# Rotary embedding worked in place in PSUM, early query and key pairs, in a two-layer decoder trunk

## The chip, the core and the metric

The kernel runs on one core of one Trainium2 chip. Its metric is the device time of one execution in microseconds (us); the median of three runs is the figure that counts. A core has TensorE (PE in the profile), VectorE (DVE), ScalarE (ACT), GpSimd (POOL) and SyncE (SP), which here only issues DMAs. Each works through its own instructions in order and waits on semaphores for the others. SBUF is the working memory; PSUM is the small memory into which TensorE writes, cut here into eight banks of 128 x 512 fp32.

## What is computed

The reference is a two-layer decoder over 512 tokens of width 1024, in fp32. Layer 0 (even) has four differential and eight forgetting attention heads. Layer 1 (odd) is a sparse attention: a light indexer scores all causal keys, each query keeps its 128 best, and 16 heads attend over those. Both layers end in a squared-ReLU MLP. Cut to what the change touches:

```python
def partial_rope(x, cos, sin):                 # first 16 of 64 dims of a head
    x1, x2, xp = xf[..., :half], xf[..., half:ROT_DIM], xf[..., ROT_DIM:]
    return concatenate([x1 * cos - x2 * sin, x2 * cos + x1 * sin, xp])
...
q, k, v, iq, ik, iw = _split(h @ w_in, ODD_WIDTHS)      # odd layer
ik = partial_rope(layernorm(ik, ln_g, ln_b))
logits = einsum('bqhd,bkd->bqhk', iq, ik) * IDX_DIM ** -0.5
score = einsum('bqhk,bqh->bqk', relu(logits), iw)
_, idx = lax.top_k(score, k_sel)
```

## The kernel before, in words

**Products.** Every fp32 matrix is split into a high part (a cast to fp32r on ACT) and a low part (a subtraction on DVE, or on POOL for some weights): `split`, lines 174 to 176. A projection of one block of 128 output columns is 24 matmuls of 128x512: high by high, high by low, low by high for each of eight slices of the depth (`gemm_steps`, lines 348 to 350). Its result stands in a PSUM bank of the ring `pg`, which has three banks (`B_PG`); the third block after it takes the same bank, once every instruction that reads it is over. Weights come as `raw` tiles over SP's queue in the order of a list (`full_plan`), two such tiles in flight, and are split when the block before is begun.

**Rope.** A query or key block is finished in `qk_fin` (402). `rope_from` (379) makes a copy with the rows swapped (stream_shuffle, 381), multiplies the block by the cosines (382) and the copy by the sines (383), and adds (384), all on DVE; `csr` holds the tables, already scaled by the token's norm (235). Then `split` makes the high and low parts, and `halves` (400) moves 64-row halves between tiles by DMAs on SP's queue, so that two heads can be multiplied side by side. The layer-0 heads with rope are the first four query and four key blocks; layer 1 ropes all eight of each, four index query blocks and the index key.

**Odd layer.** `odd` (841) first projects the index key and the index weights (844), turns them to tokens (851), normalises the key tile by tile (855 to 869; the power of -1/2 runs on POOL, 865), turns it back, ropes and splits it. Then four index query blocks are projected (877). From there `weave` merges generators by their progress: the index scores (`index_steps`, four head pairs by three query tiles, in the two banks of `pS`) beside the first steps of V, then the top-k (`topk_round`, 16 rounds of a maximum of eight and a replacement on each of three query tiles, lines 905 and 906, on DVE) beside the rest of V and the first two query and key pairs (`QK_EARLY`). V blocks don't use DVE. The loop of nine follows: scores of head pair i, softmax, the product with V of pair i-1, and the projection of pair i+2. A final reordering sets each engine's order from expected times, so the order on an engine isn't wholly that of the code.

Of the kernel before, what the change touches and what calls it, by code (L numbers as in the profile page):

```python
# [14 lines left out]
OP = mybir.AluOpType  # L15
# [33 lines left out]
OD_K = [0] * 8 + [6]  # L49
IDX_COVER = 12  # L50
DVE_ODD = 6
# [5 lines left out]
def rope_rows():  # L57
    pos = np.arange(S, dtype=np.float32)
    inv = (np.float32(THETA) ** (-(np.arange(0, ROT, 2, dtype=np.float32)) / np.float32(ROT))).astype(np.float32)
    ang = (pos[None, :] * inv[:, None]).astype(np.float32).astype(np.float64)  # L60
    c, s = np.cos(ang), np.sin(ang)
    t = np.zeros((2, P, S), np.float64)
    t[0] = 1.0
    for b in (0, HD):
        t[0, b:b + 8] = c
        t[0, b + 8:b + 16] = c
        t[1, b:b + 8] = -s
        t[1, b + 8:b + 16] = s
    return t.astype(np.float32)
# [7 lines left out]
def trunk(ctx, tc, x, norm_mix, w_in_even, b_forget, lambda_q1, lambda_k1, lambda_q2, lambda_k2,  # L77
# [226 lines left out]
    def full_plan():  # L304
# [13 lines left out]
        for s in range(2):  # L318
            stage(w, 0, 3 * D + s * WC)
        for u_ in range(4):  # L320
            stage(w, 0, 2 * D + u_ * WC, lo=nc.gpsimd)
        for i in range(8):
            for a in range(2):
                stage(w, 0, a * D + i * P, P, lo=nc.gpsimd)
        out_stages(w_out_odd[0], 0, 1, nc.gpsimd)
# [52 lines left out]

    def rope_from(src, tab):
        u, v = scr(), scr()  # L380
        nc.vector.stream_shuffle(v, src, SHUF)
        nc.vector.tensor_mul(u, src, tab[:, 0])
        nc.vector.tensor_mul(v, v, tab[:, 1])  # L383
        nc.vector.tensor_add(u, u, v)
        return u

# [454 lines left out]
    def odd(ap, gh):  # L841
        w = w_in_odd[0]
        fq, fk = qk_fin(ap, True, False), qk_fin(ap, True, True)
        iwt = wnext(w, 0, 3 * D + S)
# [5 lines left out]
        for t in range(NT):  # L850
            nc.tensor.transpose(p[:, t * P:t * P + HD + 8], ikf[:HD + 8, t * P:(t + 1) * P], ident[:HD + 8, :HD + 8])
        iw = ap.tile([P, NT, 8], F32, name="iw")
        xh = scr()
        pk = pT()
        for t in range(NT):
            rt = rtm[:, t:t + 1]
            nc.vector.tensor_scalar(iw[:, t], p[:, t * P + HD:t * P + HD + 8], rt, 8 ** -0.5, op0=OP.mult, op1=OP.mult)
            kr = small(HD)
            nc.vector.tensor_scalar(kr, p[:, t * P:t * P + HD], rt, None, op0=OP.mult)
            b6 = small(6)  # L860
            mv = small(4)
            nc.vector.bn_stats(b6, kr)
            nc.vector.bn_aggr(mv[:, 0:2], b6)
            nc.vector.tensor_scalar(mv[:, 2:3], mv[:, 1:2], EPS, None, op0=OP.add)
            nc.gpsimd.tensor_tensor(mv[:, 3:4], mv[:, 2:3], nhalf[:, 0:1], op=OP.pow)
            for s in range(2):
                nc.vector.tensor_scalar(xh[:, t * P + s * HD:t * P + (s + 1) * HD], kr, mv[:, 0:1], mv[:, 3:4],
                                        op0=OP.subtract, op1=OP.mult)
            nc.tensor.transpose(pk[:, t * P:(t + 1) * P], xh[:, t * P:(t + 1) * P], ident)
        kl = scr()  # L870
        nc.vector.tensor_scalar(kl, pk, cols[:, 41:42], cols[:, 42:43], op0=OP.mult, op1=OP.add)
        cs = blk("P", 4, (P, 2, S), pool=ap)
        nc.gpsimd.dma_start(cs, rope.rearrange("a p s -> p a s"))
        ky = rope_from(kl, cs)
        ikb = (blk("qk", QK_BUFS, dt=F32R, pool=ap), blk("qk", QK_BUFS, dt=F32R, pool=ap))
        split(ikb[0], ikb[1], ky)
        iq = proj(w, gh, 3 * D, fq) + proj(w, gh, 3 * D + WC, fq)

# [6 lines left out]
        def index_steps():  # L885
            for hp in range(4):
                for t in range(1, NT):
                    wd = (t + 1) * P
                    a = sc[t - 1]
                    sp = [pS(), pS()]  # L890
                    for m in range(2):
                        nc.tensor.matmul(sp[m][:, :wd], iq[hp][m][:, t * P:wd], ikb[0][:, :wd], start=True, stop=False)
                        nc.tensor.matmul(sp[m][:, :wd], iq[hp][m][:, t * P:wd], ikb[1][:, :wd], start=False, stop=True)
                    for m in range(2):
                        rl = scr()
                        nc.scalar.activation(rl[:, :wd], sp[m][:, :wd], AF.Relu, scale=HD ** -0.5)
                        nc.vector.scalar_tensor_tensor(a, rl[:, :wd], iw[:, t, 2 * hp + m:2 * hp + m + 1], a,  # L897
                                                       op0=OP.mult, op1=OP.add)
# [13 lines left out]
        vfin = v_fin(ap, 9, False, True)  # L912
        vs, qs, ks, res = [], [], [], []

# [3 lines left out]

        def v_steps():
            for i in range(8):  # L920
                yield from block_steps(w, gh, 2 * D + i * P, vfin, vs.append)
# [6 lines left out]
        def chain(*gens):  # L928
            for g in gens:
                yield from g  # L930

        def take(g, n):
            for _ in range(n):
                if next(g, g) is g:
                    return
                yield

        first = chain(v_steps(), *(qk_steps(i) for i in range(QK_EARLY)))
        weave((take(first, IDX_COVER), IDX_COVER), (index_steps(), 12))
        weave((first, 72 + 18 * QK_EARLY - IDX_COVER), (topk_steps(), 16))  # L940
        while vlate:
# [64 lines left out]
```

## Time and profile before

| | us |
|---|---|
| median of three runs (lowest, highest) | 1295.77 (1295.64, 1297.23) |
| profiled execution: time | 1293.84 |
| profiled execution: span of the instructions | 1292.1 |
| TensorE busy | 1259.1 |
| VectorE busy | 751.8 |
| ScalarE busy | 559.3 |
| GpSimd busy | 107.8 |

The odd layer's own stretch runs from about 616 us (index key projection) to about 900. The rows of the profile give start and duration in us, engine, line and operation, then what is written, an arrow, and what is read; the bracket at the end of a row holds the engine's idle time before it and what ended that. Group rows give count, busy time in us, mean duration in ns, and idle time before.

### The profile page before, as it was taken

Reading aid. Unit: us, or ns where it says so; the run is one execution under the profiler, and the core shown is the slowest. Engines: PE = TensorE matmul, PEld = TensorE weight load, DVE = VectorE, ACT = ScalarE, POOL = GpSimd, SP = SyncE. Lnnn points to the kernel's source line nnn. Section 1 sums busy time; section 2 is a strip of 40 time slices with the busy share of each in tenths; the row PEclk is TensorE's granted clock in tenths of the full one; section 3 lists DMA queues with packets and bytes.
Section 4 is the critical chain, followed back from the end, with each engine's and each line's share of the span. In section 5 each row is a group of like instructions: output and inputs, shape, how many; then the busy total and the mean of one; then the engine's idle time right before and its main releaser. Section 6 shows DMA issues by size and latency. Waiting matters only on the chain.

```text
span 1292.1 us, 15546 instructions
## 1 busy us (share of the span) xinstructions
PE 1259.1 (97%) x5874; PEld 1032.5 (80%) x5874; DVE 751.8 (58%) x1397; ACT 559.3 (43%) x1013; POOL 107.8 (8%) x80
## 2 busy tenths in 40 slices
PE   7999999999999999999989899999999999999998
PEld 6878888888888888888778677777888888888887
DVE  7997569464422344343789978888654332444233
ACT  5556667353311233332255258686443311333232
POOL 2000000000000000000326422230000000000000
PEclk9999999999999999999989899999999999999999
DMA  8645453333222233233241454532333223332211
GB/s 261 148 127 133 111 139 103 98 98 98 98 99 94 90 94 102 100 114 126 92 113 52 125 139 100 145 94 97 99 98 98 98 98 98 98 98 98 98 65 65
DMA packets 145898, 138.92 MB, mean 108 GB/s; under 512 B 7480, under 2 KB 130528, under 8 KB 145824
## 3 DMA queue, kind: packets, MB, share of 16 engines
q1 hardware_dynamic: 144576, 136.14, 35.4%
q10 hardware_dynamic: 720, 1.12, 0.3%
q0 software_dynamic: 528, 0.67, 0.3%
q8 instruction: 46, 0.75, 0.2%
q14 instruction: 28, 0.23, 0.1%
HBM read 111.18 MB, written 6.29 MB: 91 GB/s over the span
## 4 chain that ended last, share of the span: by engine, by line
PE 76%; DVE 14%; ACT 5%; issue 2%; DMA 2%; POOL 0%; SPq 0%; DVEq 0%; POOLq 0%; ACTq 0%
PE pg L348 23%; PE pg L350 23%; PE pg L349 23%; DVE sel L906 2%; ACT P L479 2%; DVE sm L905 2%; DVE scr L383 2%; PE pT L505 1%; DVE sel L897 1%; DVE PT L176 1%; DMA raw<-in_w_in_even_dram 1%; ACT P L492 1%; DVE qk L176 1%; DMA qk<-qk 1%; PE pS L471 1%
## 5 line engine op out<-in xcount | busy, mean ns | idle before, releaser
L175 ACT CAST whl<-raw 128x1024 fp32r<-128x1024 f32 (+1 forms) x198 | 206.4, 1044 | 528.4 <-PE pg L350 479.8
L348 PE MATMUL pg<-gh,whl 128*128 128x512 f32 x1064 | 423.7, 399 | 2.8 <-ACT whl L175 2.4
L349 PE MATMUL pg<-gh,whl 128*128 128x512 f32 x1064 | 417.8, 393 | 0.0
L350 PE MATMUL pg<-gh,whl 128*128 128x512 f32 x1064 | 417.6, 393 | 0.0
L176 DVE TENSOR_TENSOR whl<-raw,whl 128x1024 fp32r<-128x1024 f32 x172 | 209.1, 1216 | 180.9 <-ACT whl L175 180.6
L348 PEld LDWEIGHTS pg<-gh,whl 128*128 128x128 f32 x1064 | 201.0, 189 | 42.0 <-ACT whl L175 2.8
L350 PEld LDWEIGHTS pg<-gh,whl 128*128 128x128 f32 x1064 | 200.9, 189 | 41.7
L349 PEld LDWEIGHTS pg<-gh,whl 128*128 128x128 f32 x1064 | 201.2, 189 | 38.4 <-DVE gh L176 0.2
L348 PE MATMUL pg<-act,whl 128*128 128x512 f32 (+1 forms) x528 | 204.6, 388 | 0.0
L350 PE MATMUL pg<-act,whl 128*128 128x512 f32 (+1 forms) x528 | 203.4, 385 | 0.0
L349 PE MATMUL pg<-act,whl 128*128 128x512 f32 (+1 forms) x528 | 201.6, 382 | 0.0
L680 DVE SCALAR_TENSOR_TENSOR t<-pg,r_b 128x512 f32<-128x512 f32 x64 | 44.3, 692 | 156.2 <-PE pg L350 153.7
L350 PEld LDWEIGHTS pg<-act,whl 128*128 128x128 f32 x528 | 99.1, 188 | 21.8
L349 PEld LDWEIGHTS pg<-act,whl 128*128 128x128 f32 x528 | 99.2, 188 | 20.7
L348 PEld LDWEIGHTS pg<-act,whl 128*128 128x128 f32 x528 | 99.4, 188 | 18.5
L479 ACT ACTIVATE P<-P,sm 128x128 f32<-128x128 f32 (+3 forms) x128 | 71.6, 560 | 64.8 <-DVE sm L477 64.3
L633 DVE TENSOR_TENSOR h<-h,pg 128x512 f32<-128x512 f32 x46 | 31.4, 688 | 108.3 <-PE pg L350 108.3
L176 POOL TENSOR_TENSOR whl<-raw,whl 128x1024 fp32r<-128x1024 f32 x26 | 63.4, 2438 | 135.4 <-ACT whl L175 135.4
L186 POOL TENSOR_TENSOR sm<-sm,nhalf 128x4 f32<-128x4 f32 (+1 forms) x9 | 10.4, 1153 | 643.4 <-DVE sm L184 643.4
L176 DVE TENSOR_TENSOR PT<-pT,PT 128x384 fp32r<-128x384 f32 (+1 forms) x84 | 49.7, 596 | 16.7 <-ACT PT L175 16.2
L505 PE MATMUL pT<-ident,P 128*128 128x128 f32 x280 | 50.1, 280 | 7.8 <-DVE PT L176 4.2
L505 PEld LDWEIGHTS pT<-ident,P 128*128 128x128 f32 x280 | 34.0, 140 | 23.8 <-DVE PT L176 8.5
(211 smaller groups left out, 1225.3 us busy)
## 6 DMA issues: line engine op xcount, KB each, us to landing
raw<-in_w_mlp_in_dram SPq DMA_DIRECT2D x32, 1024.0 KB, 5.4
raw<-in_w_mlp_out_dram SPq DMA_DIRECT2D x32, 1024.0 KB, 4.8
qk<-qk SPq DMA_DIRECT2D x156, 128.0 KB, 2.3
raw<-in_w_in_even_dram SPq DMA_DIRECT2D x24, 512.0 KB, 4.3
raw<-in_w_in_odd_dram SPq DMA_DIRECT2D x16, 512.0 KB, 3.6
raw<-in_w_in_odd_dram SPq DMA_DIRECT2D x6, 1024.0 KB, 5.0
raw<-in_w_out_even_dram SPq DMA_DIRECT2D x4, 1024.0 KB, 5.3
h<-hd SPq DMA_DIRECT2D x16, 256.0 KB, 4.8
```

Source lines behind the costliest of these rows:

```text
L175: nc.scalar.copy(dst_hi, src)
L176: (eng or nc.vector).tensor_sub(dst_lo, src, dst_hi.bitcast(F32))
L348: nc.tensor.matmul(pout, wt[:, 0, k, :n], a, start=start and k == 0, stop=False)
L349: nc.tensor.matmul(pout, wt[:, 0, k, :n], b, start=False, stop=False)
L350: last_mm[0] = nc.tensor.matmul(pout, wt[:, 1, k, :n], a, start=False, stop=stop and k == KB - 1)
L383: nc.vector.tensor_mul(v, v, tab[:, 1])
L479: nc.scalar.activation(o, o, AF.Exp, bias=st[m][:, t:t + 1], scale=-1.0, accum_out=st[m][:, 4 + t:5 + t])
L505: nc.tensor.transpose(p[:, o - o0 + (t - kt) * P:o - o0 + (t - kt + 1) * P], pt[:, OFF[t] + kt * P:OFF[t] + (kt + 1) * P], ident)
L633: nc.vector.tensor_add(h[j], h[j], p)
L680: nc.vector.scalar_tensor_tensor(t, p, 0.0, r_b, op0=OP.max, op1=OP.mult)
L905: nc.vector.max(m8, a)
L906: nc.vector.match_replace(a, m8, a, NEG_SEL)
```

## The change

Four things. (1) `rope_from` multiplies the block by the sines first, into SBUF, and swaps the rows of that product; the sines' signs are exchanged in the table to match. The cosines' product and the sum are then written into the block's own PSUM bank, which `split` reads. The index key takes the same path without its copy to SBUF. (2) The indexer's relu on ACT writes back into its PSUM bank instead of SBUF, and the scores of every other tile use a bank of `pT` and the one of `pO`. (3) The index key's normalisation is done for the four token tiles together, with one power on POOL. (4) Three index query blocks are projected ahead of the index scores and the fourth beside them, together with two V blocks; the first two query and key pairs follow, ahead of the other six V blocks, beside the top-k. The first V weights' low part moves from POOL to DVE.

```diff
--- before.py
+++ after.py
@@ -47,7 +47,7 @@
 CUTS = (0, 2, 4)
 EV_K = [0] * 8 + [6]
 OD_K = [0] * 8 + [6]
-IDX_COVER = 12
+V_FIRST = 2
 DVE_ODD = 6
 DVE_EVEN = 6
 SHUF = list(range(8, 16)) + list(range(0, 8)) + list(range(16, 32))
@@ -64,8 +64,8 @@
     for b in (0, HD):
         t[0, b:b + 8] = c
         t[0, b + 8:b + 16] = c
-        t[1, b:b + 8] = -s
-        t[1, b + 8:b + 16] = s
+        t[1, b:b + 8] = s
+        t[1, b + 8:b + 16] = -s
     return t.astype(np.float32)
 
 
@@ -317,11 +317,14 @@
         stage(w, 0, 3 * D + S, HD + 8)
         for s in range(2):
             stage(w, 0, 3 * D + s * WC)
-        for u_ in range(4):
-            stage(w, 0, 2 * D + u_ * WC, lo=nc.gpsimd)
-        for i in range(8):
-            for a in range(2):
-                stage(w, 0, a * D + i * P, P, lo=nc.gpsimd)
+        qk = lambda i: [stage(w, 0, a * D + i * P, P, lo=nc.gpsimd) for a in range(2)]
+        for i in range(4):
+            stage(w, 0, 2 * D + i * WC, lo=nc.gpsimd if i else None)
+            if i == 0:
+                for j in range(QK_EARLY):
+                    qk(j)
+        for i in range(QK_EARLY, 8):
+            qk(i)
         out_stages(w_out_odd[0], 0, 1, nc.gpsimd)
         mlp_stages(1)
 
@@ -376,13 +379,14 @@
         fin(p, put)
         yield
 
-    def rope_from(src, tab):
+    def rope_from(p, tab):
+
         u, v = scr(), scr()
-        nc.vector.stream_shuffle(v, src, SHUF)
-        nc.vector.tensor_mul(u, src, tab[:, 0])
-        nc.vector.tensor_mul(v, v, tab[:, 1])
-        nc.vector.tensor_add(u, u, v)
-        return u
+        nc.vector.tensor_mul(u, p, tab[:, 1])
+        nc.vector.stream_shuffle(v, u, SHUF)
+        nc.vector.tensor_mul(p, p, tab[:, 0])
+        nc.vector.tensor_add(p, p, v)
+        return p
 
     def proj(w, gh, c0, fin):
         r = []
@@ -840,7 +844,7 @@
 
     def odd(ap, gh):
         w = w_in_odd[0]
-        fq, fk = qk_fin(ap, True, False), qk_fin(ap, True, True)
+        fq = qk_fin(ap, True, False)
         iwt = wnext(w, 0, 3 * D + S)
         p = pg()
         gemm(p[:HD + 8], iwt, gh, HD + 8)
@@ -849,32 +853,32 @@
         p = pT()
         for t in range(NT):
             nc.tensor.transpose(p[:, t * P:t * P + HD + 8], ikf[:HD + 8, t * P:(t + 1) * P], ident[:HD + 8, :HD + 8])
+        pt = p.rearrange("p (t c) -> p t c", c=P)
         iw = ap.tile([P, NT, 8], F32, name="iw")
+        kr = scr()[:, :NT * HD].rearrange("p (t c) -> p t c", c=HD)
+        nc.vector.tensor_tensor(kr, pt[:, :, :HD], rtm[:, :, None].to_broadcast([P, NT, HD]), op=OP.mult)
+        nc.vector.scalar_tensor_tensor(iw, pt[:, :, HD:HD + 8], 8 ** -0.5, rtm[:, :, None].to_broadcast([P, NT, 8]),
+                                       op0=OP.mult, op1=OP.mult)
+        mv, sd = small(2 * NT), small(2 * NT)
+        for t in range(NT):
+            b6 = small(6)
+            nc.vector.bn_stats(b6, kr[:, t])
+            nc.vector.bn_aggr(mv[:, 2 * t:2 * t + 2], b6)
+        nc.vector.tensor_scalar(sd[:, :NT], mv[:, 1::2], EPS, None, op0=OP.add)
+        nc.gpsimd.tensor_tensor(sd[:, NT:], sd[:, :NT], nhalf, op=OP.pow)
         xh = scr()
         pk = pT()
         for t in range(NT):
-            rt = rtm[:, t:t + 1]
-            nc.vector.tensor_scalar(iw[:, t], p[:, t * P + HD:t * P + HD + 8], rt, 8 ** -0.5, op0=OP.mult, op1=OP.mult)
-            kr = small(HD)
-            nc.vector.tensor_scalar(kr, p[:, t * P:t * P + HD], rt, None, op0=OP.mult)
-            b6 = small(6)
-            mv = small(4)
-            nc.vector.bn_stats(b6, kr)
-            nc.vector.bn_aggr(mv[:, 0:2], b6)
-            nc.vector.tensor_scalar(mv[:, 2:3], mv[:, 1:2], EPS, None, op0=OP.add)
-            nc.gpsimd.tensor_tensor(mv[:, 3:4], mv[:, 2:3], nhalf[:, 0:1], op=OP.pow)
-            for s in range(2):
-                nc.vector.tensor_scalar(xh[:, t * P + s * HD:t * P + (s + 1) * HD], kr, mv[:, 0:1], mv[:, 3:4],
-                                        op0=OP.subtract, op1=OP.mult)
+            nc.vector.tensor_scalar(xh[:, t * P:(t + 1) * P].rearrange("p (s c) -> p s c", c=HD),
+                                    kr[:, t, None, :].to_broadcast([P, 2, HD]), mv[:, 2 * t:2 * t + 1],
+                                    sd[:, NT + t:NT + t + 1], op0=OP.subtract, op1=OP.mult)
             nc.tensor.transpose(pk[:, t * P:(t + 1) * P], xh[:, t * P:(t + 1) * P], ident)
-        kl = scr()
-        nc.vector.tensor_scalar(kl, pk, cols[:, 41:42], cols[:, 42:43], op0=OP.mult, op1=OP.add)
+        nc.vector.tensor_scalar(pk, pk, cols[:, 41:42], cols[:, 42:43], op0=OP.mult, op1=OP.add)
         cs = blk("P", 4, (P, 2, S), pool=ap)
         nc.gpsimd.dma_start(cs, rope.rearrange("a p s -> p a s"))
-        ky = rope_from(kl, cs)
+        ky = rope_from(pk, cs)
         ikb = (blk("qk", QK_BUFS, dt=F32R, pool=ap), blk("qk", QK_BUFS, dt=F32R, pool=ap))
         split(ikb[0], ikb[1], ky)
-        iq = proj(w, gh, 3 * D, fq) + proj(w, gh, 3 * D + WC, fq)
 
         sel = ap.tile([P, OFF[NT] - OFF[1]], F32, name="sel")
         sc = [sel[:, OFF[t] - OFF[1]:OFF[t + 1] - OFF[1]] for t in range(1, NT)]
@@ -887,14 +891,14 @@
                 for t in range(1, NT):
                     wd = (t + 1) * P
                     a = sc[t - 1]
-                    sp = [pS(), pS()]
+                    sp = [pS(), pS()] if t % 2 else [pT(), pO()]
                     for m in range(2):
                         nc.tensor.matmul(sp[m][:, :wd], iq[hp][m][:, t * P:wd], ikb[0][:, :wd], start=True, stop=False)
                         nc.tensor.matmul(sp[m][:, :wd], iq[hp][m][:, t * P:wd], ikb[1][:, :wd], start=False, stop=True)
                     for m in range(2):
-                        rl = scr()
-                        nc.scalar.activation(rl[:, :wd], sp[m][:, :wd], AF.Relu, scale=HD ** -0.5)
-                        nc.vector.scalar_tensor_tensor(a, rl[:, :wd], iw[:, t, 2 * hp + m:2 * hp + m + 1], a,
+                        rl = sp[m][:, :wd]
+                        nc.scalar.activation(rl, rl, AF.Relu, scale=HD ** -0.5)
+                        nc.vector.scalar_tensor_tensor(a, rl, iw[:, t, 2 * hp + m:2 * hp + m + 1], a,
                                                        op0=OP.mult, op1=OP.add)
                     yield
 
@@ -910,14 +914,20 @@
         biases = [tri] + sc
         obs = [None] * KB
         vfin = v_fin(ap, 9, False, True)
-        vs, qs, ks, res = [], [], [], []
+        vs, qs, ks, res, iq = [], [], [], [], []
+
+        fk = qk_fin(ap, True, True)
 
         def qk_steps(i):
             yield from block_steps(w, gh, i * P, fq, qs.append)
             yield from block_steps(w, gh, D + i * P, fk, ks.append)
 
-        def v_steps():
-            for i in range(8):
+        def iq_steps(blocks):
+            for i in blocks:
+                yield from block_steps(w, gh, 3 * D + i * P, fq, iq.append)
+
+        def v_steps(blocks):
+            for i in blocks:
                 yield from block_steps(w, gh, 2 * D + i * P, vfin, vs.append)
 
         def topk_steps():
@@ -929,15 +939,11 @@
             for g in gens:
                 yield from g
 
-        def take(g, n):
-            for _ in range(n):
-                if next(g, g) is g:
-                    return
-                yield
-
-        first = chain(v_steps(), *(qk_steps(i) for i in range(QK_EARLY)))
-        weave((take(first, IDX_COVER), IDX_COVER), (index_steps(), 12))
-        weave((first, 72 + 18 * QK_EARLY - IDX_COVER), (topk_steps(), 16))
+        for _ in iq_steps(range(3)):
+            pass
+        weave((chain(iq_steps((3,)), v_steps(range(V_FIRST))), 9 + 9 * V_FIRST), (index_steps(), 12))
+        weave((chain(*(qk_steps(i) for i in range(QK_EARLY)), v_steps(range(V_FIRST, 8))),
+               9 * (8 - V_FIRST) + 18 * QK_EARLY), (topk_steps(), 16))
         while vlate:
             vlate.pop(0)()
         early = Early(w_out_odd[0], nc.gpsimd)
```

The order of instructions shows it at three places. The numbers tell tiles apart and differ between the two programs.

SP's queue at the head of the odd layer, before: `raw` are weight loads, `qk` the halves of the first index queries (5057 to 5059 the first, 5101 to 5103 the second).

```order
L291 DMA raw_876_5151<-in_w_in_odd_dram 128x8x256
L291 DMA raw_923_5338<-in_w_in_odd_dram 128x8x256
L400 DMA qk_860_5059<-qk_858_5057 64x512
L400 DMA qk_860_5059<-qk_859_5058 64x512
L291 DMA raw_957_5489<-in_w_in_odd_dram 128x8x256
L400 DMA qk_858_5057<-qk_859_5058 64x512
L400 DMA qk_868_5103<-qk_867_5102 64x512
L400 DMA qk_868_5103<-qk_866_5101 64x512
```

The same place now (5040 to 5042 the first index query, 5084 to 5086 the second):

```order
L291 DMA raw_870_5134<-in_w_in_odd_dram 128x8x256
L291 DMA raw_897_5288<-in_w_in_odd_dram 128x8x128
L404 DMA qk_854_5042<-qk_852_5040 64x512
L404 DMA qk_854_5042<-qk_853_5041 64x512
L404 DMA qk_852_5040<-qk_853_5041 64x512
L404 DMA qk_862_5086<-qk_860_5084 64x512
L404 DMA qk_862_5086<-qk_861_5085 64x512
L404 DMA qk_869_5128<-qk_867_5126 64x512
L404 DMA qk_860_5084<-qk_861_5085 64x512
```

One weight load stood between the second and the third transfer of the first index query; now the halves of the first three index queries follow each other, and the next load stands behind them.

DVE at the start of the even layer, before, from the scaling of the tables (`csr`): `pg_19_177` is the first query block, whose bank the fourth block takes, `pg_65_341` the first key block.

```order
L235 TENSOR_TENSOR csr_96<-csr_96,r_b_97 128x512 x2
L382 TENSOR_TENSOR scr_58_322<-pg_19_177,csr_96 128x512
L383 TENSOR_TENSOR scr_59_323<-scr_59_323,csr_96 128x512
L381 STREAM_SHUFFLE scr_67_367<-pg_65_341 128x512
L384 TENSOR_TENSOR scr_58_322<-scr_58_322,scr_59_323 128x512
L382 TENSOR_TENSOR scr_66_366<-pg_65_341,csr_96 128x512
L383 TENSOR_TENSOR scr_67_367<-scr_67_367,csr_96 128x512
L176 TENSOR_TENSOR qk_61_329<-scr_58_322,qk_60_328 128x512
L384 TENSOR_TENSOR scr_66_366<-scr_66_366,scr_67_367 128x512
```

And now:

```order
L235 TENSOR_TENSOR csr_96<-csr_96,r_b_97 128x512 x2
L385 TENSOR_TENSOR scr_58_322<-pg_19_177,csr_96 128x512
L387 TENSOR_TENSOR pg_19_177<-pg_19_177,csr_96 128x512
L386 STREAM_SHUFFLE scr_59_323<-scr_58_322 128x512
L385 TENSOR_TENSOR scr_66_366<-pg_65_341,csr_96 128x512
L388 TENSOR_TENSOR pg_19_177<-pg_19_177,scr_59_323 128x512
L386 STREAM_SHUFFLE scr_67_367<-scr_66_366 128x512
L387 TENSOR_TENSOR pg_65_341<-pg_65_341,csr_96 128x512
L176 TENSOR_TENSOR qk_61_329<-pg_19_177,qk_60_328 128x512
```

The last instruction that reads the first query block's bank was L382, one row behind the tables; now it is the split (L176 of `pg_19_177`), eight rows behind them.

DVE in the top-k of the odd layer (MAX and MATCH_REPLACE on `sel`), before, at its second and third rounds:

```order
L905 MAX sm8_951_5457<-sel_5195 128x8
L905 MAX sm8_952_5460<-sel_5195 128x8
L906 MATCH_REPLACE sel_5195<-sm8_951_5457,sel_5195 128x384
L906 MATCH_REPLACE sel_5195<-sm8_952_5460,sel_5195 128x512
L905 MAX sm8_954_5480<-sel_5195 128x8
L905 MAX sm8_955_5483<-sel_5195 128x8
L906 MATCH_REPLACE sel_5195<-sm8_954_5480,sel_5195 128x256
L906 MATCH_REPLACE sel_5195<-sm8_955_5483,sel_5195 128x384
```

And now, at the third round:

```order
L910 MATCH_REPLACE sel_5001<-sm8_922_5428,sel_5001 128x384
L910 MATCH_REPLACE sel_5001<-sm8_923_5431,sel_5001 128x512
L385 TENSOR_TENSOR scr_924_5434<-pg_914_5378,csr_96 128x512
L387 TENSOR_TENSOR pg_914_5378<-pg_914_5378,csr_96 128x512
L386 STREAM_SHUFFLE scr_925_5435<-scr_924_5434 128x512
L909 MAX sm8_932_5469<-sel_5001 128x8
L388 TENSOR_TENSOR pg_914_5378<-pg_914_5378,scr_925_5435 128x512
L910 MATCH_REPLACE sel_5001<-sm8_932_5469,sel_5001 128x256
L909 MAX sm8_933_5472<-sel_5001 128x8
L176 TENSOR_TENSOR qk_927_5441<-pg_914_5378,qk_926_5440 128x512
```

The first query block's rope (L385 to L388) and its split now stand between the rounds; before, the top-k ran without them until its last rounds.

## The prediction

> **What bounds the kernel now.** I read the first page, then what TensorE waits for, then the granted clock in the stretches behind those waits, and last the DVE groups of the odd layer.
>
> ```profile
> span 1292.1 us, 15546 instructions
> PE 1259.1 (97%) x5874; PEld 1032.5 (80%) x5874; DVE 751.8 (58%) x1397; ACT 559.3 (43%) x1013; POOL 107.8 (8%) x80
> ...
> PE pT L505 <- DVE PT L176: 4.2, 6, 1.3
> PE pS L471 <- DMA qk<-qk: 4.1, 1, 4.1
> PE pS L892 <- DMA qk<-qk: 3.6, 1, 3.6
> PE pT L505 <- ACT P L492: 3.0, 9, 1.2
> PE pg L348 <- ACT whl L175: 2.4, 1, 2.4
> PE pS L472 <- DMA qk<-qk: 1.5, 1, 1.5
> ```
>
> TensorE is busy for 97% of the span, so the change can win only what TensorE loses. Five of these six waits lie in the odd layer, the only place where the change takes work off the path. A wait costs more than its idle time:
>
> ```profile
> 570.00:580.00 10.00, 10.00 (x45) 8.23 (x44) 4.41 (x5) 3.24 (x4) 0.00 (x0) 1.00 0.35 125
> 12.60:16.00 3.40, 3.40 (x12) 2.81 (x10) 3.15 (x10) 2.04 (x5) 0.00 (x0) 0.50 1.06 287
> 655.60:661.10 5.50, 5.46 (x16) 4.81 (x17) 3.41 (x6) 2.16 (x5) 0.00 (x0) 0.50 0.69 160
> 738.00:746.40 8.40, 6.89 (x18) 5.26 (x19) 5.61 (x11) 2.84 (x7) 2.35 (x1) 0.50 0.78 209
> ...
> 651.67 0.39 PE L350 MATMUL pg<-gh,whl 128*128 128x512 f32 x1
> 655.64 0.55 PE L892 MATMUL pS<-qk,qk 128*128 128x256 f32 x1 [3.58 <-DMA qk<-qk]
> ```
>
> In the windows the clock stands third from the end: 1.00 undisturbed (44 whole matmuls in 10 us, one per 0.227 us), 0.50 behind each long wait. Half a stretch at 0.50 is lost. From start to start the wait for the index scores took 3.97 us, 0.16 more than idle and one step, which I add to every wait. The odd head thus loses 3.6 + 0.16 (index scores), 2.75 (half of 5.5), 4.1 + 1.5 + 0.3 (first pair of the loop) and 3.45 (half of 8.4 - 1.5): 15.9 us. Why the first came:
>
> ```profile
> 644.59 3.23 SPq L400 DMA_DIRECT2D qk<-qk  x2
> 647.91 0.54 SPq L291 DMA_DIRECT2D raw<-in_w_in_odd_dram  x1
> 648.50 11.48 SPq L400 DMA_DIRECT2D qk<-qk  x10
> ...
> 626.31 0.23 DVE L857 TENSOR_SCALAR iw<-pT,rtm 128x8 f32<-128x8 f32 x1 [0.78 <-PE pT L851]
> 635.93 0.81 DVE L871 TENSOR_SCALAR scr<-pT,cols 128x512 f32<-128x512 f32 x1 [0.42 <-PE pT L869]
> ```
>
> The index query's halves stood on SP behind a 1 MB weight load, and its rope stood on DVE behind a key chain of 9.6 us. On DVE itself:
>
> ```profile
> 649.62 2.41 POOL L176 TENSOR_TENSOR whl<-raw,whl 128x1024 fp32r<-128x1024 f32 x1 [3.44 <-ACT whl L175]
> 649.68 2.89 DVE L383 TENSOR_TENSOR scr<-scr,csr 128x512 f32<-128x512 f32 x1
> ...
> L383 DVE TENSOR_TENSOR scr<-scr,csr 128x512 f32<-128x512 f32 x19 | 30.2, 1592 | 0.0
> L176 DVE TENSOR_TENSOR qk<-scr,qk 128x512 fp32r<-128x512 f32 x20 | 21.4, 1070 | 7.6 <-ACT qk L175 7.6
> L382 DVE TENSOR_TENSOR scr<-pg,csr 128x512 f32<-128x512 f32 x19 | 12.8, 672 | 0.0
> L897 DVE SCALAR_TENSOR_TENSOR sel<-scr,iw,sel 128x384 f32<-128x384 f32 x8 | 4.9, 614 | 1.1 <-ACT scr L896 0.8
> ...
> L383 DVE TENSOR_TENSOR scr<-scr,csr 128x512 f32<-128x512 f32 x8 | 5.5, 685 | 0.0
> ```
>
> The first four groups are of the odd layer, the last of the even one, where POOL is idle. The same multiplication takes 685 ns there and 1592 here, and the one that starts 0.06 us after a POOL split ends just behind it. L382, whose first operand lies in PSUM, stays at 672. So a DVE instruction with two SBUF operands waits for a running POOL instruction, and one with a PSUM operand does not.
>
> **Part by part.** *Rope in PSUM.* Four DVE instructions stay four, but none has two SBUF operands (the shuffle has one input), and the split behind it subtracts from PSUM too. Nothing in the trace shows a DVE write to PSUM. Its bounds: nothing (reads: 672 against 685) and the 0.13 by which L871 (0.81) stands above L382. I take nothing. [...]
>
> *A bank held longer.* Before, the PSUM bank came free after L382; now the whole rope and both halves of its split must be over. Three banks serve the projections, so the fourth block waits for the first:
>
> ```profile
> 26.83 1.21 DVE L743 TENSOR_TENSOR pick<-ident 128x1024 fp32r<-128x1024 f32 x1
> ...
> 28.61 1.20 DVE L176 TENSOR_TENSOR whl<-raw,whl 128x1024 fp32r<-128x1024 f32 x1
> 29.73 1.28 DVE L235 TENSOR_TENSOR csr<-csr,r_b 128x512 f32<-128x512 f32 x2
> 30.93 0.68 DVE L382 TENSOR_TENSOR scr<-pg,csr 128x512 f32<-128x512 f32 x1
> ...
> 32.07 0.50 PE L348 MATMUL pg<-gh,whl 128*128 128x512 f32 x1
> ```
>
> At 32.07 TensorE began the fourth block, 0.5 us after L382 let go of the first. In the new order the sines' and cosines' scaling ends near 30.3; eight instructions at 0.6 (two such rows stand between 29.73 and 30.93) follow, the eighth being the split of the first query, so the bank is free near 35.2. Everything later on TensorE is queued behind: 3.1 + 0.16 us, and the even layer has no slack that gives them back. A half clock follows: behind 2.4 us of wait it held 3.4 us (12.6 to 16.0), behind 3.6 us 5.5, so 1.7 to 2.75 lost; I take 2.2. Cost: 5.4, between 3.1 (no half clock) and 6.7. [...] Later blocks of the even layer start well after their bank's split.
>
> *Head of the odd layer.*
>
> ```profile
> L186 POOL TENSOR_TENSOR sm<-sm,nhalf 128x4 f32<-128x4 f32 x1 | 1.0, 1040 | 0.7 <-DVE sm L184 0.7
> ...
> qk<-qk SPq DMA_DIRECT2D x156, 128.0 KB, 2.3
> ```
>
> Per key tile one scaling, one pow on POOL and a return trip go. In their place stand, by my estimates from the same instructions' rows, one scaling (0.35), the two csr rows (1.2), the gate (0.25), the statistics (1.2), one pow of 128x4 (1.0, as L186, and two hand-overs of 0.1), four subtractions (1.0) and the last transpose (0.4): about 5.7 instead of 9.6. The key's rope ends near 636.4, the first index query's near 638.8, its split 640.6. Its halves have no load ahead of them any more; the last is issued 0.7 after the split and lands 2.3 later, near 643.6. TensorE has then done three index blocks and 11 matmuls of the fourth, at 644.1. So the 3.6 goes, with its half clock. What is late next is the fourth index query: its last half stands on SP behind two 0.5 MB loads, which wait for V's weight split on DVE (1.2) near 656; I put its landing at 664, and TensorE there at 662.8. Cost 1.3, between 0 and 4.7 (3 and a half clock).
>
> *Query and key pairs early.* From 644.1 TensorE has 304 projection matmuls (69.0), 28 transposes (0.11 each: 3.1) and the index scores (48 of 384 columns on average: 8.2) before the loop's first scores: 724.4, with the 1.3 near 726. The DVE:
>
> ```profile
> 690.03 1.05 DVE sm L905 x2
> 695.95 1.05 DVE sm L905 x2
> ```
>
> Two top-k rounds take 5.92. From 647.2, when three index ropes are done: 24 additions (14.7, at 0.6 for the middle width), one rope (3.0), V's split (1.2), 16 rounds (47.4), four ropes (12.1), and about 3 of waiting for TensorE: 728.6. The scores need the selection only when their two banks are full, near 732. So the waits for 4.1 and 1.5 and the half clock behind them go, with 3 to 4 us of cover. Head: 15.9 - 1.3 = 14.5 won; bounds 8 and 16.
>
> *The loop.*
>
> ```profile
> 760.00:862.00 102.00, 94.87 (x487) 76.06 (x485) 88.59 (x185) 76.54 (x183) 30.26 (x14) 1.00 0.46 120
> ...
> PE pT L505 <- DVE PT L176: 3.6, 5, 1.3
> PE pT L505 <- ACT P L492: 3.0, 9, 1.2
> ...
> 788.30 2.61 DVE scr L383
> 808.90 2.62 DVE scr L383
> ```
>
> An iteration takes 20.6 us. DVE's held L383 (2.6 for 0.7) and held split stand ahead of the PT splits, and of the score reductions behind which ACT normalises. With 3.3 us of DVE released per iteration I expect nearly all of 6.6 + 14 x 0.16 = 8.8 to go: 8. Bounds: 0, if ACT's own chain sets the pace, and 14, if steps that the trace doesn't call waits shrink too (102 us hold five iterations; their steps at the undisturbed rate make 18).
>
> **Sum.** The profiled execution took 1293.84 (span 1292.1): + 5.4 - 14.5 - 8 = 1276.7. The median of the runs shown is 1295.77, 1.9 above it; so 1278.6, about 1278. About 0.2% (2.6 us) is what a measurement can tell from no change.
>
> **Rivals.** (a) *The loop gains nothing*: ACT is busy for 76.5 of 102 us there, and its normalisation is one of the two releasers. For it: DVE waits for ACT's casts (7.6 idle). Against: ACT itself waits for reductions behind the held rows. 1278.6 + 8 = 1286.6. Chance 20%. (b) *Everything gives way*: no half clock at the start, no wait for the fourth index query, the loop at its bound: 1295.8 + 3.3 - 15.9 - 14 = 1269. Chance 15%. (c) *Banks bind in the top-k stage* (slower): a rope's five instructions now queue between top-k rounds while holding a bank. From the sum, the third early block is split near 688 and TensorE wants its bank near 696. If DVE runs 8 us later than I count, four blocks wait like the start's (4 x 5.4) and the loop's first pair is late again (9.4 not won): 1278.6 + 21.6 + 9.4 = 1309.6. For it: DVE is full there; against: the released 3.3 us per pair. Chance 4%. (d) *DVE writes to PSUM are held by POOL after all*, so the change does not do what it says: loop and half of the head stay, 1278.6 + 8 + 7 = 1293.6, no difference. Chance 3%; L382 speaks against it. Mine has 58%.
>
> Range: from (b) with 4 us for what the bounds leave out to just above (a): 1265 to 1290. Faster: 58 + 20 + 15 = 93%; same 3%; slower 4%.
>
> **What would show it.** Right: a TensorE wait of about 3 us near 32 us for a DVE split, clock 0.50 behind it; no wait for DMA before the first index scores; rope instructions at 0.7 beside POOL; loop iterations of about 19 us. Wrong: PSUM-writing rows well above 0.7, waits on banks near 690, or iterations still at 20.6.

## The result

The changed kernel takes 1272.78 us (median of four runs, 1271.27 to 1273.33) against 1295.73 for the kernel before in the same comparison (four runs, 1295.64 to 1297.23): a ratio of 0.9818, 95% interval 0.9801 to 0.9835. The prediction was 1278, with a range of 1265 to 1290. The profiled execution took 1272.94.

The first page of the changed kernel and its waits of TensorE (line, releaser, us in total, times, longest):

```profile
span 1271.1 us, 15506 instructions
PE 1248.2 (98%) x5874; PEld 1031.1 (81%) x5874; DVE 723.1 (57%) x1386; ACT 558.1 (44%) x1013; POOL 99.9 (8%) x75
```

```profile
PE pg L252 <- DMA xw<-in_x_dram: 5.0, 1, 5.0
PE pg L351 <- DVE qk L176: 3.8, 1, 3.8
PE pg L351 <- ACT whl L175: 3.7, 2, 2.4
PE pT L875 <- DVE scr L872: 1.1, 1, 1.1
PE pT L509 <- ACT P L496: 0.8, 2, 0.5
PE pT L509 <- DVE PT L176: 0.6, 1, 0.6
PE pS L475 <- DVE sm L481: 0.6, 1, 0.6
```

The waits for `qk` halves are gone; those for PT splits shrank from 4.2 to 0.6, those for ACT's normalisation (`P`) from 3.0 to 0.8. New are the wait of 3.8 for the split of a query (even layer) and, as the second of the waits for a weight's cast (`whl`), one of 1.3 near 880 us. The two other small ones (1.1 and 0.6) were 0.7 and 0.5 before. The clock, third from the end of each row of the windows:

```profile
35.70:42.50 6.80, 6.21 (x15) 4.87 (x16) 6.61 (x18) 1.28 (x3) 0.00 (x0) 0.50 0.68 157
...
655.60:661.10 5.50, 5.50 (x29) 4.70 (x28) 4.88 (x10) 3.35 (x6) 2.41 (x1) 1.00 0.34 80
738.00:746.40 8.40, 7.87 (x37) 6.72 (x38) 6.09 (x20) 5.13 (x15) 3.71 (x2) 1.00 0.33 91
760.00:862.00 102.00, 100.92 (x555) 85.28 (x555) 83.74 (x224) 86.53 (x212) 26.92 (x14) 1.00 0.43 115
```

Both stretches at 0.50 in the odd layer are at 1.00 now, and one of 6.8 us stands at the start of the even layer. The stretch of 3.4 us near 12 us, behind the first wait for a cast, stands in both profiles. Three moments that exist in both kernels cut the time into stretches: the matmul of L204 that spreads the norm at the odd layer's start, the first scores of the loop, and L204 again ahead of the odd layer's MLP. Behind the last of them both kernels need the same time, 354.7 us. TensorE's timeline before:

```profile
624.24 0.50 PE L204 MATMUL pT<-scr,onesr 128*128 128x512 f32 x1 [0.15 <-ACT scr L175]
...
738.00 0.66 PE L471 MATMUL pS<-qk,qk 128*128 128x128 f32 x2 [4.11 <-DMA qk<-qk]
...
937.35 0.50 PE L204 MATMUL pT<-scr,onesr 128*128 128x512 f32 x1
```

And after:

```profile
632.15 0.50 PE L204 MATMUL pT<-scr,onesr 128*128 128x512 f32 x1
...
733.27 0.22 PE L475 MATMUL pS<-qk,qk 128*128 128x128 f32 x1
...
916.45 0.50 PE L204 MATMUL pT<-scr,onesr 128*128 128x512 f32 x1
```

So the even layer takes 7.9 us more (632.15 - 624.24), the head of the odd layer 12.6 less (101.12 for 113.76), first scores and loop 16.2 less (183.18 for 199.35): together 20.9 less, as much as the two profiled executions differ.

**Rope.** The DVE groups of the odd layer (640 to 860 us), as in the prediction (busy us, mean ns, idle):

```profile
...
L388 DVE TENSOR_TENSOR pg<-pg,scr 128x512 f32<-128x512 f32 x20 | 13.9, 693 | 0.0
L387 DVE TENSOR_TENSOR pg<-pg,csr 128x512 f32<-128x512 f32 x20 | 13.9, 693 | 0.0
L176 DVE TENSOR_TENSOR qk<-pg,qk 128x512 fp32r<-128x512 f32 x20 | 13.7, 685 | 4.5 <-ACT qk L175 4.5
L385 DVE TENSOR_TENSOR scr<-pg,csr 128x512 f32<-128x512 f32 x20 | 13.6, 682 | 2.3 <-PE pg L353 2.0
...
L901 DVE SCALAR_TENSOR_TENSOR sel<-pS,iw,sel 128x512 f32<-128x512 f32 x8 | 6.0, 746 | 0.8 <-ACT pS L900 0.7
```

No row of a rope or of its split is held any more: the sines' product takes 682 ns for 1592, the split 685 for 1070. The rows that also write to PSUM take 693, 11 ns more than the one that only reads it. Two rope shuffles one iteration apart in the loop (each iteration has two of them):

```profile
803.04 0.74 DVE L386 STREAM_SHUFFLE scr<-scr 128x512 f32<-128x512 f32 x1
...
821.42 0.75 DVE L386 STREAM_SHUFFLE scr<-scr 128x512 f32<-128x512 f32 x1
```

An iteration takes 18.4 us where it took 20.6.

**The start of the even layer**, on DVE and on TensorE:

```profile
28.84 1.23 DVE L176 TENSOR_TENSOR whl<-raw,whl 128x1024 fp32r<-128x1024 f32 x1 [0.37 <-ACT whl L175]
...
31.31 0.69 DVE L385 TENSOR_TENSOR scr<-pg,csr 128x512 f32<-128x512 f32 x1
...
35.55 0.68 DVE L176 TENSOR_TENSOR qk<-pg,qk 128x512 fp32r<-128x512 f32 x1
```

```profile
36.29 0.80 PE L351 MATMUL pg<-gh,whl 128*128 128x512 f32 x1 [3.81 <-DVE qk L176]
```

The fourth block starts when the first query's split lets go of its bank.

### The profile page after: what moved, and what is told of

It is laid out like the page before. It is cut to its first block, busy times and chain, and to the rows that moved or that the text cites. A ratio compares the mean times of both kernels' runs of the same rounds, so it can differ in the third digit from the quotient of the medians.

```text
span 1271.1 us, 15506 instructions
## 1 busy us (share of the span) xinstructions
PE 1248.2 (98%) x5874; PEld 1031.1 (81%) x5874; DVE 723.1 (57%) x1386; ACT 558.1 (44%) x1013; POOL 99.9 (8%) x75
## 4 chain that ended last, share of the span: by engine, by line
PE 84%; DVE 10%; ACT 3%; issue 1%; DMA 1%; POOL 0%; SPq 0%; POOLq 0%; DVEq 0%; ACTq 0%
PE pg L351 25%; PE pg L353 25%; PE pg L352 25%; DVE sel L910 2%; PE pT L509 2%; DVE sm L909 2%; PE pS L475 1%; PE pS L476 1%; ACT P L483 1%; PE pO L528 1%; PE pO L527 1%; DVE P L481 1%; DMA raw<-in_w_in_even_dram 1%; DVE PT L176 1%; DVE scr L386 1%
## 5 line engine op out<-in xcount | busy, mean ns | idle before, releaser
L176 DVE TENSOR_TENSOR whl<-raw,whl 128x1024 fp32r<-128x1024 f32 x174 | 211.5, 1216 | 182.0 <-ACT whl L175 181.6
L352 PEld LDWEIGHTS pg<-act,whl 128*128 128x128 f32 x528 | 99.1, 188 | 20.9
L176 POOL TENSOR_TENSOR whl<-raw,whl 128x1024 fp32r<-128x1024 f32 x24 | 57.8, 2407 | 123.2 <-ACT whl L175 101.6
L176 DVE TENSOR_TENSOR PT<-pT,PT 128x384 fp32r<-128x384 f32 (+1 forms) x84 | 49.8, 597 | 19.1 <-ACT PT L175 18.4
L175 ACT CAST PT<-pT 128x384 fp32r<-128x384 f32 (+1 forms) x84 | 42.5, 511 | 14.3 <-PE pT L509 13.8
L509 PE MATMUL pT<-ident,P 128*128 128x128 f32 x280 | 46.5, 275 | 1.7 <-ACT P L496 0.8
```

The lines of the kernel that those rows point to most:

```text
L175: nc.scalar.copy(dst_hi, src)
L176: (eng or nc.vector).tensor_sub(dst_lo, src, dst_hi.bitcast(F32))
L352: nc.tensor.matmul(pout, wt[:, 0, k, :n], b, start=False, stop=False)
L509: nc.tensor.transpose(p[:, o - o0 + (t - kt) * P:o - o0 + (t - kt + 1) * P], pt[:, OFF[t] + kt * P:OFF[t] + (kt + 1) * P], ident)
```

## The experiments

Theory: the gain of the odd layer is that of DVE instructions no longer held by POOL, that of the shorter key chain and that of the early pairs; the even layer pays for the bank that is held longer. Each kernel undoes one part of the change or does one alone. Every kernel computes the whole reference. The three stretches of every profiled execution in us, read off as above (the even layer's with all that is ahead of it; a stretch of 3.4 us at half clock near 12 us stands in the profiles of before, after, 5 and 10 and not in the others):

| kernel | even layer | head | first scores and loop |
|---|---|---|---|
| before | 624.2 | 113.8 | 199.4 |
| after | 632.2 | 101.1 | 183.2 |
| 1, even layer in SBUF | 626.6 | 101.0 | 183.2 |
| 2, rope in place alone | 626.0 | 112.9 | 188.0 |
| 3, all ropes in SBUF | 625.6 | 101.9 | 192.9 |
| 4, POOL's splits on DVE | 628.3 | 114.1 | 187.0 |
| 5, relu to SBUF | 630.5 | 105.1 | 184.4 |
| 6, key chain as before | 630.6 | 108.1 | 184.0 |
| 7, V ahead of the pairs | 628.5 | 101.8 | 187.5 |
| 8, after again | 631.1 | 101.0 | 183.2 |
| 9, bank free earlier | 625.4 | 100.9 | 183.2 |
| 10, as 1, again | 625.6 | 101.0 | 183.2 |

**1. The even layer's product and sum in SBUF** (after, with one edit):

```diff
-    def rope_from(p, tab):
+    def rope_from(p, tab, out=None):
...
-        nc.vector.tensor_mul(p, p, tab[:, 0])
-        nc.vector.tensor_add(p, p, v)
-        return p
+        y = p if out is None else out()
+        nc.vector.tensor_mul(y, p, tab[:, 0])
+        nc.vector.tensor_add(y, y, v)
+        return y
...
-        fq = [qk_fin(ap, r, False) for r in (True, False)]
-        fk = [qk_fin(ap, r, True) for r in (True, False)]
+        fq = [qk_fin(ap, r, False, scr) for r in (True, False)]
+        fk = [qk_fin(ap, r, True, scr) for r in (True, False)]
```

> The changed kernel, but in the even layer the cosines' product and the sum go to SBUF, so that a block's bank comes free after two multiplications. Theory (the bank is what TensorE waits for at the start): the 3.8 us wait near 32 us and the half clock of 6.8 us behind it (3.4 lost) go, 1272.8 - 7 = 1266. Rival (the even layer takes such a wait back later, or the DVE's tables are late anyhow): 1272 to 1273, with a wait at the same place.

Measured 1266.97 (ratio to before 0.9781, 0.9768 to 0.9794). Of the wait of 3.8 this is left, for the cosines' product, and no half clock follows:

```profile
PE pg L351 <- DVE scr L388: 0.6, 1, 0.6
```

So the bank explains most of the even layer's loss: 5.5 of the 7.9 us are back. The 2.4 that are left (1.1 to 1.8 in kernels 2, 3, 9 and 10) stay open; the wait of 0.6 is only a part. Where POOL is idle, work in PSUM has no gain to set against a bank held longer: the sum with two SBUF operands took 683 ns there before (L384), and in PSUM it takes 693.

**2. Rope in place alone**: before, with `rope_from` and the table's signs of the change, the even layer as in 1; key chain, relu and order as before.

> The kernel before, with the rope in place in PSUM for the odd layer's blocks alone (even layer: sum in SBUF); order, key chain and relu as before. Theory (DVE instructions with two SBUF operands wait for POOL, and that set the pace of the loop): the loop's iterations fall from 20.6 to about 18.2 us, 1295.7 - 14 = about 1281; the waits for the halves before the index scores and the loop stay. Rival (the gain is the order's alone): 1294 to 1296, iterations of 20.6.

Measured 1285.32 (0.9921, 0.9908 to 0.9935): a gain, but 4 us less than I expected. Its waits:

```profile
PE pg L348 <- DVE qk L176: 4.1, 1, 4.1
PE pS L474 <- DMA qk<-qk: 3.5, 2, 2.7
...
PE pS L473 <- DMA qk<-qk: 3.0, 1, 3.0
```

The loop is rid of its losses. (The shuffles of two iterations stand 18.4 us apart.) But in the head the bank binds: the fourth index query block waits 4.1 for the first's split, which stands behind the slow key chain. The key itself lies in SBUF here, so the products and the sum of its rope have two SBUF operands. And the pairs still come late. So rope in place alone wins the loop, but only 0.9 us in the head.

**3. All ropes' product and sum in SBUF** (after, with `y = scr()` in the place of `p` in both layers):

> The changed kernel with its order, key chain and relu, but every rope's cosine product and sum in SBUF, so that the sum has two SBUF operands again, and so has the split behind it. Theory: the head's gain of some 16 us stays, the wait at the start of the even layer is not there, and the loop loses part of its gain (two of the three held instructions are back): about 1266 + 9 = 1275. Rival (order alone): 1266.

Measured 1276.39 (0.9853, 0.984 to 0.9867). The DVE groups of the odd layer:

```profile
L176 DVE TENSOR_TENSOR qk<-scr,qk 128x512 fp32r<-128x512 f32 x21 | 22.1, 1052 | 5.7 <-ACT qk L175 5.6
L389 DVE TENSOR_TENSOR scr<-scr,scr 128x512 f32<-128x512 f32 x20 | 20.8, 1042 | 0.0
...
L388 DVE TENSOR_TENSOR scr<-pg,csr 128x512 f32<-128x512 f32 x19 | 12.8, 675 | 0.0
```

Sum and split, with both operands in SBUF, are held again (1042, 1052); the product that reads PSUM isn't. First scores and loop grow by 9.7 us, the head by 0.8. An iteration takes 19.6 us for 18.4. Some 3 of the 9.7 lie ahead of that: TensorE waits 1.9 for the selection (0.6 in the changed kernel), and half clock for 3.4 us follows.

**4. POOL's splits on DVE**: before, with the low parts of the last twelve query and key weights on DVE, so that DVE has more work and POOL almost none in the loop:

```diff
-                stage(w, 0, a * D + i * P, P, lo=nc.gpsimd)
+                stage(w, 0, a * D + i * P, P, lo=nc.gpsimd if i < QK_EARLY else None)
```

> The kernel before, with the low parts of the last twelve query and key weight blocks of the odd layer on DVE instead of POOL: POOL is idle in the loop, DVE has 2 x 1.2 us more work per iteration. Theory (POOL holds DVE): L383 back at 0.7 and L176 of qk at 0.7 in the loop, iterations of about 19 us, 1295.7 - 8 = about 1288. Rival (the DVE's work, not the hold, sets the pace): iterations longer than 20.6, 1297 to 1305.

Measured 1283.51 (0.9911, 0.9898 to 0.9925). The loop gains as much as with rope in place (again 18.4 us an iteration), though DVE got twelve splits of 1.22 us more. Between 760 and 830 us POOL has no instruction, and the two groups that took 1809 and 1542 ns there before are:

```profile
L176 DVE TENSOR_TENSOR qk<-scr,qk 128x512 fp32r<-128x512 f32 x8 | 5.5, 685 | 0.0
...
L383 DVE TENSOR_TENSOR scr<-scr,csr 128x512 f32<-128x512 f32 x8 | 5.4, 679 | 0.0
```

What is left are the head's waits:

```profile
PE pS L471 <- DMA qk<-qk: 5.6, 1, 5.6
...
PE pS L892 <- DMA qk<-qk: 3.0, 1, 3.0
```

So it was the hold by POOL, not the amount of DVE's work, that slowed the loop. The gain is some 4 us more than I expected. The even layer's 4.1 us more than before lie ahead of the weights that the edit moves: a wait of 1.2 near 83 us and one of 0.5 near 104, with half clock behind the second (last section).

**5. Relu back to SBUF**, scores in the two banks of `pS` alone (after):

```diff
-                    sp = [pS(), pS()] if t % 2 else [pT(), pO()]
+                    sp = [pS(), pS()]
...
-                        rl = sp[m][:, :wd]
-                        nc.scalar.activation(rl, rl, AF.Relu, scale=HD ** -0.5)
+                        rl = scr()[:, :wd]
+                        nc.scalar.activation(rl, sp[m][:, :wd], AF.Relu, scale=HD ** -0.5)
```

> The changed kernel with the indexer's relu written to SBUF again and its scores in the two banks of pS alone. Theory: the additions have two SBUF operands again, so those that meet a POOL split wait (before: 0.8 and 1.1 us on average instead of 0.48 and 0.75), and two banks instead of five tie TensorE to DVE; the index stage of some 20 us grows by 3 to 5 us, of which the top-k's cover of 3 to 4 us takes some: 1273 to 1277. Rival (the cover takes it all): 1272 to 1273.

Measured 1277.38 (0.9858, 0.9843 to 0.9873); the head takes 4.0 longer. DVE between 648 and 680, and TensorE's waits between 640 and 700, where the changed kernel has none:

```profile
L901 DVE SCALAR_TENSOR_TENSOR sel<-scr,iw,sel 128x512 f32<-128x512 f32 x7 | 9.6, 1370 | 0.6 <-ACT scr L900 0.6
```

```profile
PE pS L896 <- DMA qk<-qk: 1.7, 1, 1.7
PE pS L896 <- ACT scr L900: 1.1, 2, 0.7
```

The additions are held (1370 for 746), and the halves of an index query come later behind them. The edit takes back two things, the relu's place and the other banks; no run here parts them.

**6. Key chain tile by tile, as before** (after, with the old lines of `odd` from the index weights to the transposes):

> The changed kernel with the index key normalised tile by tile as before, four powers on POOL. Theory: the key chain ends 2.8 us later, the first index query's halves land near 646.5 for a TensorE that is there at 644: a wait of 2 to 3 us and perhaps a half clock, 1274 to 1278. Rival (hidden, since the first index scores stand behind three and a half blocks): 1272 to 1273.

Measured 1279.44 (0.9871, 0.9856 to 0.9886). I expected its cost as a wait for the halves; most of it came elsewhere. TensorE's timeline:

```profile
648.34 0.39 PE L353 MATMUL pg<-gh,whl 128*128 128x512 f32 x1
651.12 0.50 PE L351 MATMUL pg<-gh,whl 128*128 128x512 f32 x1 [2.40 <-DVE qk L176]
...
651.93 0.63 PE L351 MATMUL pg<-gh,whl 128*128 128x512 f32 x1
```

It is the bank again, as in 2: the fourth index query block waits for the first one's split, and half clock follows (0.63 a matmul). The wait for halves is there too, but at 1.7 the smaller.

**7. All of V ahead of the early pairs** (after, with the two generators and the two groups of loads exchanged; here the generators):

```diff
-        weave((chain(*(qk_steps(i) for i in range(QK_EARLY)), v_steps(range(V_FIRST, 8))),
+        weave((chain(v_steps(range(V_FIRST, 8)), *(qk_steps(i) for i in range(QK_EARLY))),
```

> The changed kernel with all of V ahead of the first two query and key pairs, in the weights' order too, as before the change. Theory: the pairs' ropes then come when the top-k ends, and the loop's first scores wait for their halves: 4 to 6 us of wait and a half clock of 3.5 come back, 1279 to 1283. Rival (rope in PSUM alone makes the pairs early enough): 1272 to 1275.

Measured 1275.57 (0.9849, 0.9833 to 0.9865): less loss than I expected. Its waits, and the clock between 30 and 43 us and about the first pair:

```profile
PE pS L473 <- DMA qk<-qk: 3.5, 2, 2.5
...
PE pg L348 <- DVE qk L176: 2.7, 1, 2.7
```

```profile
30.00:43.00 13.00, 10.25 (x46) 8.13 (x45) 12.93 (x31) 3.92 (x6) 0.00 (x0) 1.00 0.57 135
733.00:738.00 5.00, 4.29 (x12) 3.41 (x13) 1.80 (x6) 1.47 (x5) 0.45 (x1) 0.66 0.71 185
```

The pairs are late again and cost 5 us in the odd layer (0.7 and 4.3 in the table). But the even layer is 3.6 shorter than in the changed kernel's profile: its wait was 2.7 for 3.8 and had no half clock behind it. No run shows that the edit, which touches the odd layer alone, does this; so the changed kernel stands once more among the next three.

**8, 9, 10. The changed kernel again, the bank freed earlier, and kernel 1 again**, on one chip. Kernel 9 is kernel 1 with, in the even layer, both products ahead of the shuffle:

```diff
         nc.vector.tensor_mul(u, p, tab[:, 1])
-        nc.vector.stream_shuffle(v, u, SHUF)
         y = p if out is None else out()
+        if out is None:
+            nc.vector.stream_shuffle(v, u, SHUF)
         nc.vector.tensor_mul(y, p, tab[:, 0])
+        if out is not None:
+            nc.vector.stream_shuffle(v, u, SHUF)
```

> The changed kernel itself, run beside the two below. My theory: the wait of about 3.8 us at the start of the even layer returns in every execution, while the half clock behind it comes in zero to two stretches of 3.4 us, by where the wait falls against them. Time 1271 to 1275; wait 3.5 to 4.0 us. Rival: wait and half clock are fixed by the kernel, and this profile shows again two stretches behind the wait, 6.8 us at 0.50.

> The changed kernel with the even layer's cosine product and sum in SBUF, and there both multiplications ahead of the shuffle, so that the bank comes free one DVE instruction (0.6 us) earlier. My theory of the bank: the last 0.6 us of wait for the first query's bank goes, and the time is 0.6 us lower than that of the next kernel at most, 1266 to 1267. Rival: something else is due at the same moment (the weights' split of the fourth block), the wait changes its releaser and the time is the same.

> The changed kernel with the even layer's cosine product and sum in SBUF, again, now on the same chip as the changed kernel itself. My theory, that the start costs the changed kernel 5.4 to 7.3 us and that SBUF ropes cost the even layer nothing: 5 to 7 us below the changed kernel, 1266 to 1268. Rival, that the first difference of 5.8 us lay between chips: less than 2 us below it.

Measured 1271.51 (8; 0.9812, 0.9798 to 0.9826), 1265.90 (9; 0.9769, 0.9755 to 0.9782) and 1266.95 (10; 0.9775, 0.9762 to 0.9789). The start of the even layer in 8, TensorE's timeline:

```profile
36.76 0.51 PE L351 MATMUL pg<-gh,whl 128*128 128x512 f32 x1 [3.88 <-DVE qk L176]
...
40.05 0.62 PE L353 MATMUL pg<-gh,whl 128*128 128x512 f32 x1
40.48 0.42 PE L351 MATMUL pg<-gh,whl 128*128 128x512 f32 x1
```

The wait is the same as in the first execution, the half clock ends at 40.5 instead of 42.5. So one execution has two stretches of 3.4 us, another one. Kernel 10 is 4.6 us below kernel 8, a little less than the 5 to 7 expected. In 9 the wait of 0.5 to 0.6 for the bank is gone; the row of the fourth block's start has no bracket:

```profile
32.52 0.50 PE L351 MATMUL pg<-gh,whl 128*128 128x512 f32 x1
```

But its even layer is only 0.2 shorter than that of 10, and the intervals overlap: these two are not told apart. Either beats the changed kernel.

## Why the prediction was right, and where its sizes were off

The direction came as argued, and so did the mechanism of each of the three terms: a wait for a bank at the start, DMA waits gone from the head, DVE no longer held in the loop. The terms were + 5.4, - 14.5 and - 8, and the stretches show about + 7.9, - 17 and - 12. All three sizes were off; that the time came out 5 us from the forecast is in part luck, since the misses partly cancel. (The sum itself holds but for rounding: 15.9 less 1.3 is 14.6, and 1278.6 was put as 1278.)

- **A bank held longer: 5.4 predicted, 7.9 measured.** The eight instructions took 4.9 us (31.31 to 36.23), as counted; they began 1.0 later than I put them, since DVE ran 0.4 behind the execution of before and the weight split ahead of them waited 0.4 more for ACT's cast. TensorE came later too, and the wait was 3.8 for 3.1. The half clock took two stretches, 6.8 us, 3.4 lost for 2.2. So the whole lies above my bound of 6.7. I had scaled it with the wait, and that was the wrong rule: waits of 3.8, 3.9, 4.0, 3.3 and 2.7 us (after, 8, 5, 6, 7) were followed by 6.8, 3.4, 3.4, 3.4 and 0 us at half clock. Each is none, one or two stretches of 3.41 us, and in the profiles of before and after the clock changes only at whole multiples of that time from one another (last section). How many come differs between executions of one kernel: kernel 8, the changed kernel again, has one stretch. By the medians the term is smaller than 7.9, since kernels 1 and 10, which keep a wait of 0.5 to 0.6, are 5.8 and 4.6 below the changed kernel.
- **DVE writes to PSUM at no extra cost: right to 11 ns**: 693 beside the 682 of a row that only reads PSUM, and the 685 with SBUF alone where POOL is idle.
- **Head: - 14.5 predicted, about - 17 measured.** The prediction booked here also the half clock and the second wait of the first pair (3.45 + 1.5 + 0.16), of which 0.6 is left; with these 4.5 the head's 12.6 become 17.1. The 1.3 for the fourth index query did not come: TensorE has no wait between 640 and 700. The key chain took 6.2 (634.31 to 640.49), with a weight split of 1.2 among it, for my 5.7. Relu and banks are part of the change and had no term; the fifth kernel shows them worth 4.0 in the head, 2.8 of it as waits for banks and for a later index query's halves.
- **Pairs: cover of 3 to 4 us predicted.** TensorE waits 0.6 for the reductions behind the top-k: the selection was just in time, and the cover was used up. Less the even layer's 7.9 us, it was there at 730.4 for my 728.6, and TensorE wanted it near 730, not 732. One row of it, held by POOL for 1.9 us (last section), was in no sum.
- **Loop: - 8 predicted, about - 12 measured** (16.2 less the 4.5 above). Iterations of 18.4 instead of my 19. The prediction gives its 3.3 us of DVE released per iteration without a working; in the loop (760 to 862) the held product and split took 1675 and 1458 ns, which for two ropes makes 3.5 above the 685 of an unheld row. With TensorE busy for 100.9 of 102 us nothing is left there; kernels 2 and 4 reach the same pace. Rival (a), in which ACT sets it, falls: ACT went from 76.5 to 86.5 busy in the same window.
- **Rival (b)** (everything gives way) came in part: the fourth index query didn't wait and the loop came near its bound of 14, but half clock did follow at the start. The measured 1272.8 lies between its 1269 and my 1278.
- **Rival (d)** (DVE's writes held) falls with the 693; rival (c) (banks binding among the top-k) did not show: no wait on `pg` there. Banks did bind where no term had them, in the index queries, as soon as the key chain was slow (2 and 6).

Taken one at a time out of the changed kernel, in-place rope is worth 10.5 us of the odd layer, relu and banks 5.2, the key chain 7.8 and the pairs ahead of V 5.0 (sums over head and loop in the table): 28.5 together, of 28.8 gained there. That they add up so closely isn't shown to be more than chance: the sums hold half-clock stretches, which may follow a wait or not, and the rest of the new order (three index queries ahead, two V blocks beside the scores) was not undone. Rope alone, put into the kernel before, gives 12.2, of which the loop has 11.3.

## What to carry to other kernels

In these runs a DVE instruction of two tensors escaped POOL's hold as soon as one of them lay in PSUM (682 to 693 ns in the changed kernel's odd layer, where two in SBUF took 1592 and 1070 before), but work in place keeps the bank; use it where POOL runs, and SBUF where the bank is due next. When a wait on a bank or a transfer is priced, count from the instruction that is really ahead of the first one in the chain, and price half clock in whole stretches (of 3.41 us in these profiles), none, one or two. Undo each part by itself before keeping all of it: here one layer's share of a good edit cost 4.6 to 5.8 us.

## What the runs showed of the hardware

A DVE instruction with a single SBUF operand was held too. After, at the end of the top-k, on DVE and on POOL:

```profile
734.92 2.22 DVE L912 TENSOR_SCALAR sel<-sel 128x384 f32<-128x384 f32 x1
...
737.84 0.43 DVE L912 TENSOR_SCALAR sel<-sel 128x512 f32<-128x512 f32 x1
```

```profile
734.52 2.41 POOL L176 TENSOR_TENSOR whl<-raw,whl 128x1024 fp32r<-128x1024 f32 x1 [2.29 <-PE pS L476]
```

The wider of the two takes 0.43; the one that begins inside a POOL split ends 0.2 behind it. The same row took 0.35 before; in kernel 3 the row of 256 columns took 2.46, the two wider ones 0.34 and 0.43. The shuffles, the maxima and the replacements of the same stage, with all their operands in SBUF, show no such rows (0.76 at most). So my rule of two SBUF operands was too narrow. Where it isn't held, such a row is faster than a sum (0.43 for 512 columns, against 0.69); whether that has to do with the hold is not shown.

In the profile of before the granted clock falls from 1.00 to 0.50 at 12.60, 654.30 and 736.22 us and is back at 16.01, 661.13 and 746.46; in that of after it falls at 11.78 and 35.67 and is back at 15.19 and 42.50. So the stretches, but for the one that the end of the kernel cuts, last 3.41, 6.83 and 10.24 us: one, two or three times 3.413. The times between them are multiples of it too: 638.29 is 187 times and 75.09 is 22 times 3.413 (before), 20.48 is 6 times (after). Three of them begin within a wait: TensorE went on at 655.64 and 738.00 (before) and at 36.29 (after). Half clock can also follow much less idle time than above: in kernel 4 a wait of 0.5 us among narrow matmuls, near 104 us, was followed by a stretch of 3.4.

```profile
103.84 0.30 PE L471 MATMUL pS<-qk,qk 128*128 128x128 f32 x1 [0.47 <-DVE P L552]
...
106.83 0.62 PE L350 MATMUL pg<-gh,whl 128*128 128x512 f32 x1
```
